# Two more weight pairs in the front stage, joint block scores, and one sample step per unit in an encoder step

## The chip, the cores and the metric

The kernel runs on one core of a Trainium2 chip. The metric is the device time of one execution in microseconds; lower is better. All arithmetic is fp32; products that need accuracy are made of fp32r halves (a high part and a low part of each operand, three matmuls for a product).

## The reference

One step of a one-layer streaming encoder on 1024 prompt positions and 8 samples of 16 positions (T = 1152 rows, D_MODEL = 1024). Cut to what this change touches:

```python
h = rmsnorm(x, g_pre_mix)
qa, ka, va, qb, kb, vb, ga, gb = project(h, w_in)   # h @ w_in: 34 column tiles of 128
# prompt: per chunk of 64 positions, band attention with bias (and sink in branch A)
oa = prompt_band(qa, ka, va, 128, bias_a, sink)     # window 128, 8 heads, 2 kv heads
ob = prompt_band(qb, kb, vb, 512, bias_b, None)     # 8 chunks back, 8 heads
# samples: 16 new positions on a cache of 128
oa_s = sample_band(qa_s, ka_s, va_s, cache_a, bias, sink)
ob_s = sample_band(qb_s, kb_s, vb_s, cache_b, bias, None)
merged = sigmoid(ga) * (oa @ w_oa) + sigmoid(gb) * (ob @ w_ob)
```

After it come the output projection, a gated MLP with a width-3 convolution, and norms. Those stages are not touched.

## The kernel before, in words

**Front stage.** The rows of x are normalised and transposed into xk, and h @ w_in is begun. Two column tiles of w_in form a pair (list `pairs`, L196): one pair is a 2x2 block product (two tiles, two halves of the contraction, two halves of the rows) that `head`/`Away`/`head_back` and `tail` (L440 to L477) compute with seven half-size products instead of eight. A product is two row chunks of 288 columns, four contraction steps and three matmuls, 24 matmuls, so a pair is 7 x 24 = 168 matmuls of 288 columns. There are ten pairs. The first seven (`NA`) have their first two products made early (class `Away`, L222). For each operand `split_left` (L171) runs one copy on ScalarE and one subtraction on VectorE; results go to `in_dr` in HBM by `store`.

**Attention stage** (L489 to L870). The 14 column tiles that no pair holds are computed here as dense work: `dense_pieces` (L525) cuts a tile into three pieces of 384 columns, a piece into four quanta of six matmuls (24 per piece, 72 per tile). Between them stand the eight units, one pair of heads each: units 0 to 3 are branch A (two key blocks of 128 per query block), units 4 to 7 branch B (up to five). A unit has six steps: four prompt steps ("p") of two query blocks, and after the second of them two sample steps ("s"), one for each half of the samples.

A step runs in a pipeline with the one before it. Its scores (`scores` L636, `sample_scores` L723) go out first; VectorE adds the bias and takes the minimum (L666), ScalarE takes the exponent (L671), VectorE normalises (L682, L686). Meanwhile TensorE makes the transposes of the step before (L703, into two PSUM tiles `pt`, each copied out by ScalarE L707 or VectorE L705), then its products with V (`values` L712). `spread` (L812) puts the quanta of dense work between these parts, by `share` (L831) and by `pieces_per_unit` (L823): 4 pieces in units 0 to 3, then 6, 6, 6, 5. The parts of a prompt step are: first score block, two transposes, two transposes, rest of the scores and the normalising, transposes, rest, and the late transposes of samples:

```python
items = [step(sc), step(tr, 2), step(tr, 2), rest(sc), step(tr, 2), rest(tr), lates]
upto = quanta * share[i] // share[-1]
spread(items, dense, upto - done)
```

`scores` yields after each of its two query blocks (L675), so that transposes and dense work stand between the two. `fetch(u + 1)` (L602) loads the rows of the next unit at step i == 3 (L836); its splits (L557 to L561) run on ScalarE and VectorE. All loads and stores are issued from one queue (SP). A scheduler at compile time follows the order of the program and lets an engine take a later instruction where it believes that an earlier one is not ready; on the chip each engine then runs its list in order. The score tiles in PSUM are two (`pss`), of two banks each.

A sample step loads half a K cache and half a V cache (L737 to L740, one buffer each), makes 16 score matmuls (16 records), softmax on 128 x 144, two transposes (L769, L770), ten value records (L778, L781), a copy, and one step later a late transpose and a store (L785).

## Time and profile before

| | |
|---|---|
| three runs | 1658.04, 1662.12, 1663.2 us, median 1662.12 |
| the profiled execution | 1666.81 us |
| its span, first to last instruction | 1665.0 us |
| mean granted TensorE clock | 0.991 |
| TensorE matmul, weight load | 97%, 89% of the span |
| VectorE, ScalarE, GpSimd | 65%, 44%, 13% |
| DMA | 206.47 MB, mean 124 GB/s |

The profile is of one execution. Matmul records overlap, and their ends are modelled, so a time is best read from one start to the next. The attention stage begins at 256 us of the span and ends at about 616 us.

### The profile page before, as it was taken

To read this page: it belongs to the slowest core of one execution; us is meant where nothing else is said; L and a number is where in the kernel's file an instruction comes from. 1 tells how busy PE (TensorE), PEld (TensorE's weight loads), DVE (VectorE), ACT (ScalarE), POOL (GpSimd) and SP (SyncE) were. 2 spreads that over 40 slices of the span, in tenths; PEclk is the share of its full clock that TensorE was granted. 3 is DMA by queue.
4 is the path that set the end of the run, shared out by engine and by line. 5 is a ranking of instruction groups with operands and counts; after the bars stand their busy time and mean duration, and the time that the engine had idled before them with its cause. 6 is when DMAs were issued, how large, how long until landed. Compare 5 with 4: busy or idle time off the path is not lost. (4 is left out here: it accounts for less than half of the span.)

```text
span 1665.0 us, 27771 instructions
## 1 busy us (share of the span) xinstructions
PE 1609.2 (97%) x10839; PEld 1480.8 (89%) x10839; DVE 1086.8 (65%) x2009; ACT 726.6 (44%) x1417; POOL 223.8 (13%) x297
## 2 busy tenths in 40 slices
PE   6999999999999999999999999999999998999997
PEld 6999998788888889978898999999999997888886
DVE  6965546665665546454397766766666675965986
ACT  7511235565454445332373344444444444534342
POOL 1000011111111103411002211111111110000003
PEclk9999999999999999999999999999999999999999
DMA  7743326445333236442254311221221129053023
GB/s 256 246 167 143 113 83 208 141 142 163 121 116 119 72 126 229 135 161 94 76 188 128 118 64 70 80 80 71 75 80 67 68 68 339 2 194 128 1 94 134
DMA packets 95364, 206.47 MB, mean 124 GB/s; under 512 B 21704, under 2 KB 46072, under 8 KB 95232
## 3 DMA queue, kind: packets, MB, share of 16 engines
q1 hardware_dynamic: 95232, 204.69, 36.2%
q8 instruction: 85, 1.39, 0.3%
q14 instruction: 47, 0.39, 0.1%
HBM read 148.13 MB, written 61.24 MB: 126 GB/s over the span
## 5 line engine op out<-in xcount | busy, mean ns | idle before, releaser
L143 PE MATMUL x<-xot,s 128*128 128x288 f32 x1152 | 157.7, 295 | 0.9 <-DVE w L1144 0.9
L143 PEld LDWEIGHTS x<-xot,s 128*128 128x128 f32 x1152 | 154.9, 188 | 1.1 <-ACT a L1007 1.1
L1354 PE MATMUL x<-wbp,zap 128*128 128x512 f32 x576 | 135.3, 389 | 0.0
L1354 PEld LDWEIGHTS x<-wbp,zap 128*128 128x128 f32 x576 | 108.1, 188 | 22.4
L1007 ACT ACTIVATE s<-uw 128x512 fp32r<-128x512 f32 x96 | 60.1, 626 | 96.1 <-issue 41.7
L1354 PE MATMUL p<-wbp,zap 128*128 128x512 f32 x432 | 102.0, 393 | 0.0
L1354 PEld LDWEIGHTS p<-wbp,zap 128*128 128x128 f32 x432 | 82.2, 190 | 17.2
L1008 DVE TENSOR_TENSOR s<-uw,s 128x512 fp32r<-128x512 f32 x96 | 68.9, 718 | 32.3 <-ACT s L1007 32.3
L1185 DVE SCALAR_TENSOR_TENSOR wk<-w,cw,wk 128x128 f32<-128x128 f32 (+2 forms) x144 | 83.0, 613 | 9.9 <-ACT wk L1183 9.1
L671 ACT ACTIVATE p<-p,m 128x256 f32<-128x256 f32 (+4 forms) x128 | 74.9, 588 | 33.0 <-DVE m L666 33.0
L143 PE MATMUL x<-xob,s 128*128 128x288 f32 x576 | 82.6, 299 | 6.3 <-DVE wk L1144 6.3
L143 PEld LDWEIGHTS x<-xob,s 128*128 128x128 f32 x576 | 79.6, 191 | 6.9 <-ACT s L1007 2.6
L1008 DVE TENSOR_TENSOR a<-uw,a 128x512 fp32r<-128x512 f32 x62 | 42.8, 691 | 63.6 <-ACT a L1007 62.4
L143 PE MATMUL z<-xot,s 128*128 128x288 f32 x576 | 80.7, 295 | 0.0
L143 PE MATMUL z<-xot,a 128*128 128x288 f32 x576 | 80.7, 295 | 0.0
L143 PEld LDWEIGHTS z<-xot,s 128*128 128x128 f32 x576 | 78.1, 188 | 0.0
L143 PEld LDWEIGHTS z<-xot,a 128*128 128x128 f32 x576 | 78.1, 188 | 0.0
L143 PE MATMUL ix<-t,s_i 128*128 128x288 f32 x480 | 65.6, 295 | 0.3 <-DVE iu L188 0.3
L143 PEld LDWEIGHTS ix<-t,s_i 128*128 128x128 f32 x480 | 64.3, 188 | 0.5 <-issue 0.5
L143 PE MATMUL x<-xob,a 128*128 128x288 f32 x456 | 63.9, 295 | 0.0
L143 PE MATMUL y<-xob,a 128*128 128x288 f32 x456 | 63.9, 295 | 0.0
L143 PEld LDWEIGHTS x<-xob,a 128*128 128x128 f32 x456 | 61.8, 188 | 0.0
(657 smaller groups left out, 3890.9 us busy)
## 6 DMA issues: line engine op xcount, KB each, us to landing
uw<-in_w_upg SPq DMA_DIRECT2D x53, 512.0 KB, 4.5
iw<-in_w_in SPq DMA_DIRECT2D x27, 512.0 KB, 4.6
gg<-in_dr SPq DMA_DIRECT2D x16, 576.0 KB, 3.9
in_dr<-gt SPq DMA_DIRECT2D x42, 192.0 KB, 1.9
z_dr<-wk SPq DMA_DIRECT2D x24, 256.0 KB, 2.1
z_dr<-wk SPq DMA_DIRECT2D x24, 224.0 KB, 1.9
xt<-in_x SPq DMA_DIRECT2D x9, 512.0 KB, 9.9
oT<-o_dr SPq DMA_DIRECT2D x8, 576.0 KB, 7.1
```

What stands on the lines that cost most here:

```text
L143: nc.tensor.matmul(ps, w[:, i, k], right(j, c, k), start=first and n == 0, stop=last and n == len(todo) - 1, skip_group_check=True)
L671: nc.scalar.activation(p[h][:, 0:n], p[h][:, 0:n], AF.Exp, bias=least[h], scale=-1.0, accum_out=st.d[:, h, i:i + 1])
L1007: nc.scalar.activation(sp[:, 0], src, AF.Copy)
L1008: nc.vector.tensor_tensor(sp[:, 1], src, fr(sp[:, 0]), op=ALU.subtract)
L1185: nc.vector.scalar_tensor_tensor(out, src(t), cw[:, f, t:t + 1], out, op0=ALU.mult, op1=ALU.add)
L1354: nc.tensor.matmul(ps, z[:, i, k, c], w[:, j, k], start=first and n == 0, stop=last and n == 2, skip_group_check=True)
```

## The change

Tiles 6, 7 and 11, 15 leave the dense list and become two more pairs of the front stage (fifth and sixth of twelve). `dense_tiles` keeps ten tiles, 30 pieces, of which the units get 3, 3, 3, 3, 4, 4, 4, 3 and the end of the stage three, as before. `scores` no longer yields between the two query blocks, except after the first one where the keys take two chunks (third and fourth prompt steps of units 4 to 7). The two sample steps of a unit become one step, with the same matmuls, softmax operations for each half, and buffers that hold both halves: four cache tiles from three buffers, one PSUM tile for the transposes and one for the values, one copy of each. `fetch(u + 1)` stands at i == 2, ahead of the sample step. The output tile `oo` of the prompt steps has one buffer instead of two.

```diff
-        pairs = [(4, 5), (0, 1), (2, 3), (10, 14)] + [(18 + n, 26 + n) for n in range(6)]
+        pairs = [(4, 5), (0, 1), (2, 3), (10, 14), (6, 7), (11, 15)] + [(18 + n, 26 + n) for n in range(6)]
...
                 st.k0.append(k0)
-                yield
+                if i == 0 and nch > 1:
+                    yield
+            yield
...
-            o = pp.tile([P, 256], F32, name=f"oo{st.name}", tag="oo")
+            o = pp.tile([P, 256], F32, name=f"oo{st.name}", tag="oo", bufs=1)
...
-        def sample_scores(st, u, half):
+        def sample_scores(st, u):
...
-            kt = sm.tile([P, 4, P], F32, name=f"kc{st.name}", tag="kc", bufs=1)
-            nc.sync.dma_start(kt[:], kc[ci, half])
-            st.v = sm.tile([P, 4, P], F32, name=f"vc{st.name}", tag="vc", bufs=1)
-            nc.sync.dma_start(st.v[:], vc[ci, half])
+            kt, st.v = [[sm.tile([P, 4, P], F32, name=f"{n}{st.name}_{half}", tag="cache", bufs=3) for half in range(2)]
+                        for n in ("kc", "vc")]
+            for src, tiles in ((kc, kt), (vc, st.v)):
+                for half in range(2):
+                    nc.sync.dma_start(tiles[half][:], src[ci, half])
...
+            for half in range(2):
+                for i in range(4):
+                    b = half * 4 + i
...
+                    nc.tensor.matmul(ps[r, half, 0:P], q, kt[half][:, i], start=True, stop=True)
+                    nc.tensor.matmul(ps[r, half, P:144], q, k.kn[:, b * SS:(b + 1) * SS], start=True, stop=True)
...
+            pt = pst.tile([P, 2, 2, P], F32, name=f"t{st.name}", tag="pt")
+            for half in range(2):
+                nc.tensor.transpose(pt[:, half, 0], st.p[:, half, 0:P], ident[:])
+                nc.tensor.transpose(pt[:, half, 1], pms[half][:], ident[:])
...
-        dense_tiles = [6, 11, 15, 7, 12, 16, 8, 13, 17, 9, 24, 32, 25, 33]
+        dense_tiles = [12, 16, 8, 13, 17, 9, 24, 32, 25, 33]
...
-        pieces_per_unit = [4, 4, 4, 4, 6, 6, 6, 5]
+        pieces_per_unit = [3, 3, 3, 3, 4, 4, 4, 3]
...
-            order = [("p", 0), ("p", 1), ("s", 0), ("s", 1), ("p", 2), ("p", 3)]
-            share = [3, 5, 7, 9, 13, 17] if u < 4 else [3, 6, 8, 10, 14, 18]
+            order = [("p", 0), ("p", 1), ("s", None), ("p", 2), ("p", 3)]
+            share = [3, 5, 8, 12, 16] if u < 4 else [3, 6, 9, 13, 17]
...
-                if i == 3 and u < 7:
+                if i == 2 and u < 7:
                     fetch(u + 1)
```

## Rows read from the trace of the kernel before

**Rows 1.** The page's first part: busy us, share of the span, instructions.

```profile
PE 1609.2 (97%) x10839; PEld 1480.8 (89%) x10839; DVE 1086.8 (65%) x2009; ACT 726.6 (44%) x1417; POOL 223.8 (13%) x297
```

**Rows 2.** Windows, attention stage: length; busy PE, PEld, DVE, ACT, POOL; clock, DMA, GB/s.

```profile
256.00:616.00 360.00, 353.51 (x2821) 296.66 (x2820) 220.78 (x781) 181.06 (x510) 42.39 (x54) 1.00 0.40 126
```

**Rows 3.** Timeline, TensorE, end of the front stage: start, duration, instruction, count.

```profile
249.67 3.35 PE L143 MATMUL ix<-xk,s_i 128*128 128x288 f32 x24
252.86 3.35 PE L143 MATMUL iz<-t,a_i 128*128 128x288 f32 x24
256.05 0.34 PE L117 MATMUL d<-xk,w6s 128*128 128x384 f32 x1
...
257.78 0.34 PE L118 MATMUL d<-xk,w6s 128*128 128x384 f32 x1
```

**Rows 4.** Windows, single units (1, 2 and 7), columns as in rows 2.

```profile
290.80:327.90 37.10, 34.78 (x280) 28.66 (x278) 22.45 (x90) 19.97 (x66) 5.03 (x12) 0.95 0.45 134
327.90:360.60 32.70, 32.70 (x280) 27.59 (x278) 21.75 (x88) 19.52 (x65) 4.04 (x6) 1.00 0.44 141
...
552.40:598.80 46.40, 46.38 (x384) 38.76 (x382) 29.29 (x102) 22.34 (x56) 2.39 (x1) 1.00 0.18 58
```

**Rows 5.** Timeline, TensorE, pieces of steps in units 1, 2 and 4.

```profile
313.74 0.39 PE L663 MATMUL s<-kah,q1h 64*128 64x256 f32 x2
...
314.29 0.33 PE L769 MATMUL ts<-ident,ps 128*128 128x128 f32 x1
...
329.72 0.45 PE L117 MATMUL d<-xk,w15s 128*128 128x384 f32 x1
...
342.97 0.45 PE L745 MATMUL sss<-kcs,qbd 128*32 128x128 f32 x8
...
343.40 0.33 PE L769 MATMUL ts<-ident,ps 128*128 128x128 f32 x1
...
343.59 0.42 PE L117 MATMUL d<-xk,w7s 128*128 128x384 f32 x1
...
345.76 0.38 PE L778 MATMUL os<-vtna,pcs 128*128 128x128 f32 x2
346.07 0.42 PE L781 MATMUL os<-vcs,pcs 128*32 128x128 f32 x8
346.43 0.38 PE L663 MATMUL s<-kah,q2h 64*128 64x256 f32 x2
...
358.34 0.42 PE L117 MATMUL d<-xk,w7s 128*128 128x384 f32 x1
...
425.91 0.42 PE L663 MATMUL s<-k4h,q4h 64*128 64x320 f32 x2
...
426.98 0.45 PE L117 MATMUL d<-xk,w8s 128*128 128x384 f32 x1
```

**Rows 6.** Timeline, second prompt step of unit 2: scores, minimum, exponent, sink, normalising.

```profile
333.25 0.39 PE L663 MATMUL s<-kah,q2h 64*128 64x256 f32 x2
...
333.91 0.48 DVE L666 CUSTOM_DVE_ANT_0 p<-s,bt,sinkb 128x256 f32<-128x256 f32 x1
...
335.04 0.50 ACT L671 ACTIVATE p<-p,m 128x256 f32<-128x256 f32 x1
...
337.01 0.47 ACT L680 ACTIVATE se<-m,sinkp 128x2 f32<-128x2 f32 x2
...
337.93 1.14 DVE L686 TENSOR_SCALAR p<-p,dn 128x256 f32<-128x256 f32 x4
```

**Rows 7.** Timeline, two waits of TensorE and the load behind the first.

```profile
288.53 0.32 SPq L549 DMA_DIRECT2D k4raw<-in_dr  x1
...
294.13 0.63 ACT L557 ACTIVATE k4h<-k4raw 128x512 fp32r<-128x512 f32 x1 [3.74 <-DMA k4raw<-in_dr]
...
296.06 0.58 PE L703 MATMUL pt<-ident,p 128*128 128x128 f32 x2 [2.32 <-ACT pk L707]
...
448.22 0.66 PE L703 MATMUL pt<-ident,p 128*128 128x128 f32 x4 [2.47 <-DVE oo L720]
```

**Rows 8.** DMA issues of the attention stage: stores of `oo`, KB each, us to landing.

```profile
o_dr<-oo SPq DMA_DIRECT2D x32, 128.0 KB, 2.9
```

## Prediction

> **What bounds the kernel now.** I read the page's busy shares first: TensorE is busy for 97% of the span, VectorE for 65%, ScalarE for 44% [rows 1]. Then the windows by stage: in the 360 us of the attention stage TensorE is busy for 353.51 us, its weight loads for only 296.66, VectorE for 220.78, ScalarE for 181.06 [rows 2]. So the stage is TensorE's, but the records overlap, and "busy" hides what passes between two kinds of matmuls. The timeline shows it: dense matmuls follow each other every (257.78 - 256.05) / 10 = 0.173 us [rows 3], so twelve should take 2.08 us, but a visit of twelve lasts from 343.59 to 345.76, 2.17 us [rows 5]. Six score matmuls (three pairs of 256 columns, 0.12 us each by the pitch inside the group) take 313.74 to 314.29, 0.55 us [rows 5]: about 0.2 us of it is the change of operand shape. Every visit to another kind of work costs TensorE 0.1 to 0.2 us in which it counts as busy.

> [...]

> **The change part by part**, against the profiled execution (1665.0 us of span, 1666.8 in all, 4.7 us above the median of the runs).

> *Two more pairs.* Dense, two pairs are four tiles of 72 matmuls: 288 x 0.173 = 49.8 us. In the front stage they are 2 x 168 matmuls; a product of 24 lasts 252.86 - 249.67 = 3.19 us, so 2 x 7 x 3.19 = 44.7 us [rows 3]. Net **-5.1 us**. Their splits on ScalarE and VectorE, loads and stores lie beside the products as those of the ten pairs do; rows 3 show products back to back to the last. Were this cover gone, it would show there as pitch.

> *Joint scores.* Two groups of 0.55 us become one. The nearest joint group is that of two chunks of 320 columns, 425.91 to 426.98, 1.07 us [rows 5]; with 2 x 64 columns less per matmul pair I estimate 0.9 us for 256. That saves 0.2 us a step (bounds: nothing, and 0.3 if the second group cost only its pitch). Units 0 to 3 have four such steps, 0.8 us each unit, units 4 to 7 two, 0.4 us.

> *One sample step.* Scores: 0.43 us a half [rows 5], of which the pitch inside is some 0.1 to 0.2; joint about 0.6, saving 0.25. Values: 0.67 us a half (345.76 to 346.43 [rows 5]); joint about 0.9, saving 0.4. Transposes cost the same. **0.65 us** a unit (bounds 0.3 and 0.8). Softmax operations are as many; ScalarE copies, the reciprocal and the sink terms are halved, a fraction of a us off the path.

> *Fewer visits of dense work.* Unit 2 has 14 visits (the first at 329.72, the last at 358.34 [rows 5]). The program's order alone gives 10 (one in each of the first four steps, three in each of the last two); the compiler's reordering added four. After, with five steps, no break between the score blocks and 12 quanta instead of 16, the program's order gives 6; I take 8, and in units 4 to 7 five fewer by the same count. At 0.1 us: 0.6 and 0.5 us a unit.

> Sum of the merging: 4 x (0.8 + 0.65 + 0.6) + 4 x (0.4 + 0.65 + 0.5) = **-14.4 us**. Gross with the pairs: -19.5.

> *What it costs.* The dense work is also the cover of the softmax chain. In unit 2 the chain from the first score to the last normalising is 333.25 to 337.93 + 1.14 = 339.07, 5.8 us; ScalarE's four exponents (0.5 us apart) and the sink terms set its end more than the second block's scores do [rows 6], so joint scores shorten it little. The unit takes 32.7 us over six steps [rows 4], 5.4 each. After: 32.7 - 4 x 6 x 0.173 (one piece) - 2.05 = 26.5 us over five, 5.3 each. The second prompt step is left with one quantum and about 4 us of TensorE work; the transposes that need its result come after the sample scores, some 0.9 us too early. The compiler can pull quanta of the sample step forward (the four added visits above are of that kind), at 0.1 to 0.2 us for each extra visit. The four minima of a step now stand together on VectorE, 0.4 us apart, and a copy of transposes queued behind them on VectorE makes the third `pt` tile wait. I take **1 us a unit, +7** in all (one unit ends the stage); bounds 0 and 2.5. VectorE rises from 21.75 of 32.7 us [rows 4] to about 21.5 of 27.5, 78%; it does not become the bound, and unit 7, with 20 quanta instead of 24, ran its 46.4 us with TensorE busy for 46.38 [rows 4].

> *One buffer of `oo`.* The copy must now wait for the store before it, issued at once and landed 2.9 us later [rows 8]; steps are 4 us apart at least. Nothing, up to 0.5 us a unit when the store lands late; it is inside the 7. Behind the waiting copy on VectorE stand the minima of the next step, so the same bound holds for TensorE.

> *The fetch and the sample loads.* The fetch moves ahead of the eight bias and four cache loads of the sample step; in time it stays the sample step plus two prompt steps before its unit. No loads are added, and cache loads have three buffers for four tiles, so only the second V half waits for a score group, a step before it is read. What matters is a load that lands later than the compiler thought: the keys for unit 4, issued at 288.53, held ScalarE until 294.13, and TensorE, waiting for ScalarE's copy of `pt`, stood 2.32 us [rows 7]. [...] One such event costs 4.4 us; a second one, of 2.47 us, is at 448.22. They can vanish or grow in number: +-5 us, taken as 0.

> Total: -19.5 + 7 = -12.5. From the profiled 1666.8 this gives 1654; from the median 1662.1 it gives **1649.5 us**.

> **The rivals.**
> *A, nothing new waits.* The gross gain stays, and one or both late loads go: -19.5 to -25, 1637 to 1643. For it: a list scheduler with 12 free quanta a unit has enough to fill 1 us. Against: every step has less of it.
> *B, only the arithmetic counts.* If TensorE at 97% is full, no visit costs anything and only the pairs pay: -5.1, 1657. [...]
> *C, the chain takes over (slower).* The front stage grows by 44.7 us for certain; the attention stage must give that up, and gross it gives 49.8 + 14.4 = 64.2. The place is the transposes of each prompt step, waiting for the normalising 5.8 us after its scores and for the two `pt` tiles. From 19.5 us of waits on, 0.5 us in each of the 40 steps, the change loses; with 0.7 us in each (28 us) it is +8.5, **1671 us**. For it: the two longest waits of the stage are of this kind [rows 7]. Against: they had a late load behind them, and VectorE and ScalarE have idle time in every unit.
> [...] No row here shows scores waiting for a tile.
> *D, the pairs don't pay.* Seven products at the front cost what eight dense ones did, by loads or splits that fall behind, and the merging is lost in extra visits: 0, 1662. Against: the even 3.19 us [rows 3].

> **How the numbers follow.** Forecast 0.50 (1643 to 1656, from waits of 0.2 to 1.7 us a unit), A 0.17, B 0.12, C 0.13, D 0.08. Runs of this kernel differ by 0.3%, 5 us, and less can't be told from no change. Forecast and A are faster; B lies on that line and is halved; C is slower, D the same: faster 0.73, same 0.14, slower 0.13. The range, 1637 to 1662, takes in the forecast, A, B and half of D, and leaves out C.

> **What the profile would show.** Right: dense work starts at about 301 us and the stage ends near 604, 303 us long; twelve score matmuls in about 0.9 us and 32 sample score records in about 0.6; eight dense visits in unit 2 for 14; VectorE's share of the stage above 70%; waits of TensorE in it below 15 us. Wrong: long waits at the transposes behind L686, L707 or L705, or behind `oo`; a granted clock below 0.98 in the stage; products of the front further apart than 3.19 us.

## The result, and the profile after

The changed kernel takes **1643.74 us** (four runs, 1642.28 to 1648.29) beside 1662.11 for the kernel before on the same chip: ratio 0.9897, 95% interval 0.988 to 0.9915, 18 us less. The forecast was 1649.5: faster, as said, but by half as much again. In the experiments a gain in us beside a ratio is that ratio's share of the 1662 us before, which can differ by up to 2 us from the difference of two medians. The profiled execution took 1648.29 us with a span of 1646.5, 18.5 us under that of the kernel before. Both profiled executions lie 4.6 to 4.7 us above the median of their runs, so the two traces can be set against each other as they stand.

The first part of the page after, and the row of a DMA queue, q8, that becomes important later (packets, MB, share):

```profile
PE 1591.7 (97%) x10887; PEld 1471.5 (89%) x10887; DVE 1096.0 (67%) x2015; ACT 726.1 (44%) x1411; POOL 215.9 (13%) x293
...
q8 instruction: 85, 1.39, 0.3%
```

TensorE has 48 matmuls more than in [rows 1], which is 2 x 168 - 288. The windows of the attention stage and of the up-projection stage, columns as in rows 2:

```profile
300.00:603.73 303.73, 292.61 (x2535) 244.26 (x2533) 210.88 (x754) 167.62 (x478) 34.09 (x51) 1.00 0.43 138
...
819.07:1372.10 553.03, 540.23 (x4044) 538.64 (x4042) 392.61 (x619) 257.96 (x483) 103.26 (x145) 1.00 0.29 96
```

The same windows of the kernel before:

```profile
256.05:619.23 363.18, 354.07 (x2824) 296.89 (x2822) 221.85 (x782) 183.60 (x514) 42.39 (x54) 1.00 0.40 128
...
832.96:1391.10 558.14, 543.07 (x4043) 541.66 (x4041) 392.78 (x618) 257.47 (x483) 102.77 (x145) 0.99 0.28 95
```

So the front stage gives 300.0 - 256.0 = +44.0 us, the attention stage 303.7 - 363.2 = -59.5, and everything behind it -3.0, of which the up-projection stage, which the change does not touch, has -5.1. How far such differences hold is seen in the traces of the experiments below. The attention stage repeats within 0.8 us where the code is the same (363.2, 363.7 and 363.5 us before; 303.7, 303.8 and 304.0 after). The front stage, where its start is not delayed, varies more: 252.4 to 256.1 us in six traces with ten pairs, 297.4 to 300.0 in five with twelve, 44.5 apart in the mean.

The end of the front stage (timeline, TensorE), which answers to [rows 3]:

```profile
293.66 3.35 PE L143 MATMUL ix<-xk,s_i 128*128 128x288 f32 x24
296.84 3.35 PE L143 MATMUL iz<-t,a_i 128*128 128x288 f32 x24
300.03 0.34 PE L117 MATMUL d<-xk,w12s 128*128 128x384 f32 x1
```

The products still follow each other every 3.18 to 3.19 us. Pieces of steps in unit 1, which answer to [rows 5]:

```profile
336.23 0.39 PE L663 MATMUL s<-kah,q1h 64*128 64x256 f32 x2
...
337.14 0.87 PE L705 MATMUL pt<-ident,p 128*128 128x128 f32 x6
...
338.99 0.45 PE L749 MATMUL sss<-kcs,qbd 128*32 128x128 f32 x8
...
339.71 0.45 PE L117 MATMUL d<-xk,w16s 128*128 128x384 f32 x1
...
350.94 0.60 PE L786 MATMUL os<-vtna,pcs 128*128 128x128 f32 x4
...
352.04 0.39 PE L663 MATMUL s<-kah,q1h 64*128 64x256 f32 x2
```

Twelve score matmuls take 337.14 - 336.23 = 0.91 us, where two groups of 0.55 stood; the 32 records of the sample scores 0.72, where two halves of 0.43 stood; the values 1.10, where two of 0.67 stood.

The waits of TensorE in the attention stage after (us in total, times, longest):

```profile
PE pt L705 <- ACT pk L709: 2.7, 6, 0.7
PE o L720 <- ACT pk L709: 2.7, 4, 1.4
PE pt L705 <- DVE pk L707: 2.4, 1, 2.4
PE ts L777 <- DVE pm L768: 0.5, 1, 0.5
```

They sum to 8.3 us against 6.4 before. No row is behind `oo`, and none has scores waiting for a tile. The most regular of them is the third `pt` tile, here in unit 1:

```profile
331.86 0.40 ACT L671 ACTIVATE p<-p,m 128x128 f32<-128x128 f32 x1 [1.01 <-DVE m L666]
...
332.64 0.58 ACT L709 ACTIVATE pk<-pt 128x512 f32<-128x512 f32 x1
...
333.27 0.44 PE L705 MATMUL pt<-ident,p 128*128 128x128 f32 x2 [0.67 <-ACT pk L709]
```

ScalarE waits for the first minima, takes two exponents, and only then copies the `pt` tile that TensorE needs emptied. This is the place of rival C, at 0.67 us and not in every step. The longest wait, 2.42 us, has another origin:

```profile
417.05 3.49 DVE L561 SCALAR_TENSOR_TENSOR q5l<-q5raw,q5h 128x512 fp32r<-128x512 f32 x2
417.30 2.69 POOL L104 TENSOR_TENSOR w9s<-w9r,w9s 128x1024 fp32r<-128x1024 f32 x1 [1.33 <-issue]
...
422.04 0.44 PE L705 MATMUL pt<-ident,p 128*128 128x128 f32 x2 [2.42 <-DVE pk L707]
```

Two query splits, elsewhere 0.69 us each, take 3.49 us while GpSimd subtracts a weight tile, and the minima and the `pk` copy stand behind them on VectorE. Taken singly, the first lasted its usual 0.68 us; the second, begun at 417.65, lasted 2.89 us and ended 0.55 us after the subtraction, as if it had stood still until GpSimd was done.

Single units after (units 1 and 2), columns as in rows 4:

```profile
330.32:358.35 28.03, 27.24 (x254) 22.93 (x253) 21.22 (x86) 18.86 (x63) 4.90 (x12) 1.00 0.56 168
358.35:386.47 28.12, 27.11 (x254) 23.13 (x252) 20.14 (x85) 17.52 (x61) 4.38 (x7) 1.00 0.51 158
```

Unit 2 came to 28.12 us, not 27.5; unit 1 fell from 37.10 [rows 4] to 28.03, at a granted clock of 1.00 instead of 0.95.

### The profile page after: what moved, and what is told of

It reads as the page before. It is cut to its first block, busy times and chain, and to the rows that moved or that the text cites. A ratio compares the mean times of both kernels' runs of the same rounds, so it can differ in the third digit from the quotient of the medians.

```text
span 1646.5 us, 27860 instructions
## 1 busy us (share of the span) xinstructions
PE 1591.7 (97%) x10887; PEld 1471.5 (89%) x10887; DVE 1096.0 (67%) x2015; ACT 726.1 (44%) x1411; POOL 215.9 (13%) x293
## 5 line engine op out<-in xcount | busy, mean ns | idle before, releaser
L143 PE MATMUL ix<-t,s_i 128*128 128x288 f32 x576 | 78.6, 295 | 0.3 <-DVE iu L188 0.3
L143 PEld LDWEIGHTS ix<-t,s_i 128*128 128x128 f32 x576 | 77.2, 188 | 0.5 <-issue 0.5
L173 ACT ACTIVATE s_i<-iw 128x512 fp32r<-128x512 f32 x48 | 30.3, 630 | 88.4 <-PE ix L143 49.0
## 6 DMA issues: line engine op xcount, KB each, us to landing
z_dr<-wk SPq DMA_DIRECT2D x24, 256.0 KB, 2.1
xt<-in_x SPq DMA_DIRECT2D x9, 512.0 KB, 10.1
```

Source lines behind the costliest of these rows:

```text
L143: nc.tensor.matmul(ps, w[:, i, k], right(j, c, k), start=first and n == 0, stop=last and n == len(todo) - 1, skip_group_check=True)
L173: nc.scalar.activation(sp[:, 0], src, AF.Copy)
```

## The experiments

Each is compared with the kernel before on the same chip. First the parts of the change one by one.

**The pairs alone**, on the old units:

```diff
-        pairs = [(4, 5), (0, 1), (2, 3), (10, 14)] + ...
+        pairs = [(4, 5), (0, 1), (2, 3), (10, 14), (6, 7), (11, 15)] + ...
-        dense_tiles = [6, 11, 15, 7, 12, 16, ...]
-        pieces_per_unit = [4, 4, 4, 4, 6, 6, 6, 5]
+        dense_tiles = [12, 16, ...]
+        pieces_per_unit = [3, 3, 3, 3, 4, 4, 4, 3]
```

> The twelve pairs, ten dense tiles and 27 + 3 dense pieces alone, on the old six-step units (two sample steps, a yield after each score block). Theory 'the parts add up': the pairs give 5.1 us on TensorE (front +44, dense work -50) and the shorter cover costs 0 to 5 us of new waits at the transposes, so 1657 to 1662, ratio 0.997 to 1.000. Rival 'the pairs bring the gain': most of the 18 us comes with the pairs, ratio below 0.993 (under 1651). Rival 'the old steps need the cover': ratio above 1.002.

1653.34 us, ratio 0.9944 (0.9929 to 0.9959), -9.3 us: more than the theory and less than its rival had said. But the trace gives the pairs only a part of that: the front stage ends at 298.2 and the attention stage lasts 315.4 us, so both together are 613.6 against 619.2 before. The rest lies behind them: the up-projection stage lasts 550.3 us instead of 558.1, with the same instructions. That asked for the last six experiments.

**The joint scores alone**: only the `yield` of `scores` is moved.

```diff
                 st.k0.append(k0)
-                yield
+                if i == 0 and nch > 1:
+                    yield
+            yield
```

> Only the yield between the two score blocks is gone; ten pairs, six steps, old buffers. Theory 'the parts add up': 24 joint groups save 0.19 us each (4.6 us) and about 24 dense visits of 0.1 us go, less some new waits for the pt tiles: -4 to -7 us, 1655 to 1658, ratio 0.996 to 0.9975; joint groups of 256 columns last 0.91 us. Rival 'the copies behind the four minima eat it': waits of TensorE at the pt tiles grow by 4 us or more, ratio 0.999 to 1.002.

1655.74 us, 0.996 (0.9946 to 0.9974), -6.6 us. The attention stage lasts 355.3 us, 7.9 less. Unit 1 alone fell from 37.1 to 32.1, so the late load of [rows 7] no longer stops TensorE: ScalarE comes to the split of those keys 4.7 us after their load was issued, and does not wait. The rest of the stage gave 2.8 us, less than the 4.8 of the arithmetic, though its visits of dense work fell from 137 to 127.

**The one sample step alone**: the new `sample_scores` and its followers, `fetch` at i == 2, one buffer of `oo` and the five-step `share` lists; pairs, dense tiles, pieces and yields as before.

```diff
-            order = [("p", 0), ("p", 1), ("s", 0), ("s", 1), ("p", 2), ("p", 3)]
+            order = [("p", 0), ("p", 1), ("s", None), ("p", 2), ("p", 3)]
...
```

> Only the sample step made one (with its buffers, one oo buffer, five steps, the fetch at the third step, the share lists of after with the old 4 and 6 pieces); ten pairs, a yield after each score block. Theory 'the parts add up': 32 score records in 0.72 us instead of 2 x 0.42, 20 value records in 1.11 instead of 2 x 0.67, eight steps fewer with one or two dense visits each: -3 to -6 us, 1656 to 1659, ratio 0.9965 to 0.998. Rival 'the larger lump blocks': single oo buffer and one long softmax make TensorE wait, ratio at or above 1.000.

1661.91 us, 1.0003 (0.9989 to 1.0016): nothing, as the rival had said, but hardly for its reason: the two long waits of TensorE, 2.9 and 2.2 us, stand where the kernel before had 2.3 and 2.5. Units 2 and 3 last 32.7 and 34.5 us, as before; unit 0 gains 2.1 and unit 1 loses 1.1 again to the late load, which is still there (timeline of this kernel, then its window with the granted clock):

```profile
288.92 0.63 ACT L557 ACTIVATE k4h<-k4raw 128x512 fp32r<-128x512 f32 x1 [4.28 <-DMA k4raw<-in_dr]
...
290.67 0.69 PE L703 MATMUL pt<-ident,p 128*128 128x128 f32 x2 [2.92 <-DVE pk L705]
```

```profile
280.00:300.00 20.00, 17.08 (x110) 13.97 (x111) 11.23 (x41) 8.92 (x30) 1.26 (x6) 0.83 0.47 150
```

TensorE stood for 2.92 us, and the granted clock of those 20 us is 0.83.

In the kernel after the same load holds ScalarE for 0.44 us only:

```profile
335.29 1.15 ACT L557 ACTIVATE k4h<-k4raw 128x512 fp32r<-128x512 f32 x2 [0.44 <-DMA k4raw<-in_dr]
```

**Joint scores and one sample step, without the new pairs** (the two edits above together):

> Joint scores and one sample step together, without the two new pairs (ten pairs, 14 dense tiles, 4 and 6 pieces). Theory 'the parts add up': the sum of the two single edits, -8 to -13 us, 1649 to 1654, ratio 0.992 to 0.995; the attention stage is shorter by that and the front stage unchanged. Rival 'pairs and merging need each other': less than half of the 18 us (ratio above 0.9945) here and in the pairs alone. Rival 'merging is all of it': ratio 0.990 or below, with the full cover of dense work still there.

1651.69 us, 0.9939 (0.992 to 0.9959), -10.1 us. The window of its attention stage:

```profile
253.20:604.10 350.90, 341.71 (x2823) 294.78 (x2821) 216.77 (x754) 176.14 (x494) 42.05 (x54) 1.00 0.41 132
```

12.3 us less than before. Unit 2 lasts 31.5 us, 1.2 less; unit 1 5.6 less. The sample step, worth nothing alone, gives 355.3 - 350.9 = 4.4 us of this stage on top of the joint scores. ScalarE does not wait for the keys of unit 4 here either. From here to the kernel after, the stage gets 47.2 us shorter, 2.6 short of the 49.8 that the dense work takes.

**Two further pairs**, fourteen in all, on the kernel after: tiles 12, 16 and 13, 17 become pairs, and six dense tiles are left.

```diff
+        pairs = [..., (6, 7), (11, 15), (12, 16), (13, 17)] + ...
...
-        pieces_per_unit = [3, 3, 3, 3, 4, 4, 4, 3]
+        pieces_per_unit = [2, 2, 2, 2, 2, 2, 2, 1]
```

> After with two pairs more, (12, 16) and (13, 17): 14 pairs, six dense tiles, two pieces a unit (one in the last), three at the end. Theory 'the parts add up, cover still there': front +44.7, dense work -50, new waits 1 to 4 us, so front and attention stage together shrink by 1 to 4 us against after (603.7 us to the end of the attention stage). Rival 'the chain takes over' (C of the prediction): with 8 quanta a unit the transposes wait for the normalising and for the pt tiles in most steps, waits of TensorE in the attention stage above 20 us, and the two stages together grow by more than 5 us. The late stages may move by some 7 us either way by the fetch phase, so the stages are compared, not the totals alone.

1660.99 us, 0.9996 (0.9985 to 1.0008). The front stage grows by 42.7 us, as before, but the attention stage gives up only 27.2 of 49.8. Its window, and two of its waits:

```profile
342.70:619.20 276.50, 261.44 (x2248) 200.24 (x2246) 209.85 (x754) 159.82 (x462) 24.16 (x46) 0.99 0.43 137
```

```profile
PE ts L777 <- DVE pm L768: 2.6, 1, 2.6
...
PE s L663 <- DVE m L666: 1.7, 6, 0.5
```

Here the chain has taken over: VectorE is busy for 76% of the stage, and there are waits at every link of it, among them six where scores wait for the minima that free their tile, of which the kernel after had none. Named waits sum to only 12 us, not above 20 as the rival had said. The trace also has its work in smaller pieces: the score matmuls stand in 86 groups instead of 45, and a visit of dense work has 5.2 matmuls in the mean instead of 6.8. That the rest of the 22.6 us lost lies there is likely, but was not measured by itself.

**The low halves of the dense weights on VectorE instead of GpSimd**, on the kernel after:

```diff
-        box["w"] = weight_tile(w_in[col], f"w{col}")
+        box["w"] = weight_tile(w_in[col], f"w{col}", "scalar", "vector")
```

> After with the low halves of the dense weights made on VectorE instead of GpSimd (ten subtractions of 1.2 us more on VectorE, none of 2.4 to 2.7 us on GpSimd in the attention stage). Theory 'the two engines slow each other': the query split of 3.49 us beside GpSimd's subtraction at 417 us returns to 1.4, the wait of 2.42 us at the transposes after it goes, the attention stage is 0 to 4 us shorter, ratio to before 0.987 to 0.990. Rival 'VectorE is short of time': 12 us more on it bring waits at the transposes, the stage is 2 to 6 us longer, ratio 0.991 to 0.994.

1644.24 us, 0.9898 (0.9879 to 0.9917): as the kernel after. The wait of 2.4 us behind the query splits is gone (the longest of `pt` is 1.2), but VectorE has 216.4 us of work in place of 210.9, and the stage lasts 305.1 us against 303.7, where 0 to 4 us less were expected. The two query splits now take 1.28 us together instead of 3.49, so it was the subtraction on GpSimd that had held them up; by what means, no trace shows. The wait was worth removing, the work was not worth moving.

**The late stage.** This is the up-projection stage; its instructions are the same in every kernel here. SP's queue at some of its first loads (start, us, count), before and after:

```profile
911.64 2.37 SPq L1192 DMA_DIRECT2D w<-c_dr  x3
...
931.56 2.61 SPq L1192 DMA_DIRECT2D w<-c_dr  x3
```

```profile
879.19 1.35 SPq L1204 DMA_DIRECT2D w<-c_dr  x3
...
886.60 2.16 SPq L1140 DMA_DIRECT2D a<-a_dr  x2
894.09 0.32 SPq L1222 DMA_DIRECT2D z_dr<-wk  x1
...
896.64 1.36 SPq L1204 DMA_DIRECT2D w<-c_dr  x3
```

Three issues take 1.35 us after, but 2.37 and 2.61 before; one of the three is over a microsecond longer. What differs is when a packet of the queue q8 runs. In a window at the long issue before, and in one after (packets, MB, share):

```profile
q8 instruction: 1, 0.02, 8.4%
```

```profile
q8 instruction: 1, 0.02, 4.2%
```

The first is 911.6 to 912.6, on the issue; the second 889 to 891, where SP has nothing to issue. The page has 85 such packets for 2 x 10887 matmuls and weight loads, 256 for each, and in the up-projection stage 256 of TensorE's instructions start from one packet to the next in the median, before as after: so q8 brings TensorE's instruction list (kernels with 2 x 10967 have 86 packets). The pairs lengthen that list by 96 matmuls and weight loads ahead of the late stages, and so move every later fetch. The long issue reaches TensorE by a chain of waits (kernel before): ScalarE waits for the rows that it loads, VectorE for ScalarE, and TensorE for a sum that stands behind that on VectorE.

```profile
915.42 1.15 ACT L1183 ACTIVATE wk<-w,cb,cw 128x448 f32<-128x448 f32 x2 [2.85 <-DMA w<-c_dr]
916.21 0.69 DVE L1185 SCALAR_TENSOR_TENSOR wk<-w,cw,wk 128x448 f32<-128x448 f32 x1 [2.92 <-ACT wk L1183]
917.41 2.96 PE L143 MATMUL x<-xob,s 128*128 128x288 f32 x11 [2.37 <-DVE wk L1144]
```

The first 127 us of the stage, before and after:

```profile
832.96:960.00 127.04, 117.89 (x856) 116.72 (x855) 103.95 (x162) 60.40 (x100) 22.07 (x31) 0.97 0.45 142
```

```profile
819.07:946.11 127.04, 120.06 (x894) 118.71 (x893) 108.30 (x167) 63.03 (x104) 25.88 (x35) 1.00 0.47 146
```

After, TensorE is 38 matmuls further in the same time, at a granted clock of 1.00 instead of 0.97. Its waits there sum to 9.1 us before and 6.9 after; those that differ, before and then after:

```profile
PE x L143 <- DVE wk L1144: 6.3, 3, 2.4
```

```profile
PE x L143 <- DVE w L1156: 1.5, 1, 1.5
PE x L143 <- ACT wk L1195: 1.4, 1, 1.4
PE x L143 <- ACT s L1019: 1.2, 1, 1.2
```

To test this, idle matmuls were put at the very start, to shift the list and nothing else. First form: 24 (96 instructions) in the kernel before, 40 (160) in the kernel after.

```diff
+            warm = psz.tile([P, 512], F32, name="warm", tag="ps")
+            for _ in range(24):
+                nc.tensor.matmul(warm[:, 0:8], ident[:], ident[:, 0:8], start=True, stop=True)
             b = []
```

> The kernel before with 24 tiny extra matmuls (identity by eight of its columns, into a PSUM tile that nothing reads) at the very start, where TensorE waits for the first rows: 96 more instructions on TensorE, no other work. Theory 'fetch phase': the late stages run faster with the two pairs because TensorE's instruction list is longer by about 96 and its fetches no longer fall on the loads w<-c_dr of the up-projection stage; so this kernel gains what the pairs alone gained beyond 3 us: the stretch from that stage's first matmul to the down-projection falls from 556-558 to 550-553 us, in all -4 to -8 us, ratio 0.995 to 0.9975. Rival 'it is something the pairs do' (rows in memory, DMA traffic): the stretch stays at 556-558 us, ratio 0.9985 to 1.0015.

> The kernel after with 40 of the same tiny matmuls (160 instructions on TensorE), which brings its instruction list at the up-projection stage to the place, modulo 256, that the joint merging without pairs had. Theory 'fetch phase': the waits of 2 to 3 us at 65, 85 and 106 us into that stage come back, the stretch to the down-projection grows from 550-553 to 556-558 us, and the time rises by 4 to 8 us over after: ratio to before 0.992 to 0.995. Rival 'it is something the pairs do': ratio 0.9885 to 0.991, as after.

The kernel before with 96: 1662.71 us, 1.0005 (0.9993 to 1.0016); its up-projection stage fell to 551.0 us. The kernel after with 160: 1660.19, 0.9994 (0.9981 to 1.0006), its stage rose to 556.9. The stage did what was expected both times. Both totals missed what was expected, and say little, because the idle matmuls were slow (timeline of the first):

```profile
1.34 10.41 PE L312 MATMUL warm<-ident 128*128 128x8 f32 x48 [1.34 <-POOL ident masks.py:199]
11.60 3.52 PE L286 MATMUL tp<-ident,xn 128*128 128x128 f32 x16
```

The first transposes start at 11.6 us instead of 7.8, in the second kernel at 18.4. The second form loads only 8 columns and splits the idle matmuls over two places where TensorE waits for VectorE anyway:

```diff
+            for _ in range(16):
+                nc.tensor.matmul(warm[0:8, 0:8], ident[:, 0:8], ident[:, 0:8], start=True, stop=True)
             b = []
...
                 b[1].transposed()
+                for _ in range(8):
+                    nc.tensor.matmul(warm[0:8, 0:8], ident[:, 0:8], ident[:, 0:8], start=True, stop=True)
```

These are the 24 of a shift by 96; a shift by 160 has 24 and 16. The start of the first:

```profile
1.34 0.95 PE L312 MATMUL warm<-ident 128*8 128x8 f32 x32 [1.34 <-POOL ident masks.py:199]
7.86 1.97 PE L286 MATMUL tp<-ident,xn 128*128 128x128 f32 x8 [5.56 <-DVE xn L278]
```

With these the start is not delayed. Four kernels were shifted: before, merged without pairs, after, and pairs alone (96, 96, 160 and 160 instructions).

> The kernel before with 24 extra fp32 matmuls of 8 x 8 on TensorE (96 instructions), 16 ahead of the first transposes and 8 after the second block's, where TensorE waits for VectorE anyway; their results are not used. Theory of the fetch (TensorE's instruction list is fetched in blocks of 256 instructions, and where a fetch falls on a DMA issue of SP, that issue takes 1.0 to 1.7 us instead of 0.43, and the load comes late): 131 + 96 = 227 into a block when the up-projection stage starts, close to the kernel after (212), so the stage lasts 551 to 553 us instead of 558, the first loads of that stage are issued in under 0.6 us each, and the whole is 5 to 7 us faster, ratio 0.9955 to 0.997. Rival (the late stage gains only from what the pairs changed ahead of it): stage of 556 to 558, ratio 0.999 to 1.001. In the earlier form with 128 x 8 matmuls the start was 3.8 us late; here the first transposes should start by 8.5 us.

> The joint scores and the one sample step without the two new pairs, with the same 24 extra matmuls of 8 x 8 (results not used): 116 + 96 = 212 into a block, as in the kernel after. Theory of the fetch: up-projection stage of 550 to 553 us instead of 557.8, and the whole 5 to 7 us under the 1651.7 of the same kernel without them: 1645 to 1647, ratio to the kernel before 0.9895 to 0.991. Then the pairs themselves are worth 1 to 4 us, and about half of what they gave alone (9.3 us) was where the fetches fell. Rival (the pairs are worth 9 us by themselves): stage of 556 to 558, ratio 0.993 to 0.995.

> The kernel after with 40 extra fp32 matmuls of 8 x 8 (160 instructions, results not used), 24 ahead of the first transposes and 16 after the second block's: 212 + 160 = 372, 116 into a block, as in the merging without pairs. Theory of the fetch: the up-projection stage lasts 555 to 558 us instead of 550 to 553, with long issues (over 1 us) of its first loads and waits of 1.5 to 2.9 us on TensorE, and the whole loses 5 to 7 us: 1648 to 1652, ratio to the kernel before 0.9925 to 0.995, if the start is not delayed. Rival: the extra matmuls cost only their own time, 1 to 3 us where they outlast VectorE's wait: stage of 550 to 553, ratio 0.989 to 0.991.

> The two new pairs alone, on the old units of six steps, with 40 extra matmuls of 8 x 8 (160 instructions, results not used): 222 + 160 = 382, 126 into a block, where the kernel before stands (131). Theory of the fetch: up-projection stage of 555 to 559 us instead of 550.3, with issues over 1 us at the loads of a, z_dr and w; the three shifts so far moved the time by 1.8, 3.8 and 6 us, so the ratio goes from 0.9944 to between 0.9955 and 0.998 (1653 to 1658 beside 1661). Rival (the gain of the pairs alone does not hang on the fetches): stage of 550 to 553, ratio 0.9935 to 0.9955.

They took 1661.30, 1648.20, 1651.11 and 1659.02 us. Ratios to the kernel before (interval in brackets), by where the up-projection stage starts in a block of 256 instructions, and that stage's length in the profile. The place is the number of TensorE's matmuls, weight loads and semaphore instructions in the trace ahead of the stage, less whole blocks; in the four shifted kernels it came out one less than expected:

| | at 115 to 131 | at 211 to 226 |
|---|---|---|
| before | 1; 558.1 us | 0.9989 (0.9977 to 1.0002); 551.8 |
| pairs alone | 0.9988 (0.9977 to 0.9999); 555.5 | 0.9944 (0.9929 to 0.9959); 550.3 |
| merging alone | 0.9939 (0.992 to 0.9959); 557.8 | 0.9916 (0.9899 to 0.9934); 551.7 |
| both | 0.9933 (0.9916 to 0.9951); 559.4 | 0.9897 (0.988 to 0.9915); 553.0 |

In every row the right column is the faster one, by 1.8, 7.3, 3.8 and 6.0 us, 4.7 in the mean (in the first row within the interval of nothing, in the third the two intervals overlap a little), whether the idle matmuls were added on the left or on the right. Three stage lengths came as the theory of the fetch had said, and the fourth, 559.4 us for the kernel after, lies beyond the 555 to 558 expected. Of the totals only that of the kernel after came as expected: the kernel before and the merged one moved less, the pairs alone more. SP's rows go with it: the merged kernel shifted to 211, then the kernel after shifted to 115:

```profile
877.92 1.37 SPq L1209 DMA_DIRECT2D w<-c_dr  x3
```

```profile
896.75 2.69 SPq L1209 DMA_DIRECT2D w<-c_dr  x3
```

The other traces say the same. Seven of the fourteen kernels here start the stage at 115 to 131: they have three to five issues of SP over 0.9 us in its first 127 us, each on a packet of q8, and the stage lasts 555.5 to 559.4 us. The other seven have one or none, and it lasts 549.0 to 553.0 us.

The rival, that the late stage gains from what else the pairs change, has fallen: the merged kernel has no new pairs, and 24 idle matmuls give it the short stage; the kernel after has them, and 40 idle matmuls take it away. Why a fetch for TensorE holds up an issue of SP was not tried and stays open; when it does is told in the last section. Nor is it known why the kernel before gains only 1.8 us in its runs where its profiled stage is 6.3 us shorter. A part is the spread of executions: its profiled execution lies 4.7 us above the median of its runs, that of its shifted form 2.2 below.

## Why the prediction was right, and where it was not

**Right in sign and in place.** Dense work was to start at 301 us and starts at 300.03. The stage was to end near 604; that was reckoned from an end at 616 us, where the last dense matmul stands before (its record ends at 616.6), and by the same mark it ends at 601.1. The 603.73 used above is the first matmul of the next stage, at 619.23 before, so its nearness to 604 is chance. Front and attention together are -15.5 us in the trace, where -12.5 was forecast, and the rest, -3.0, was in no step. From like to like in the table, the change is worth 0.9933 on the left (-11 us) and 0.9897 / 0.9989 = 0.9908 on the right (-15 us): the forecast of -12.5 lies between them. What it missed is the fetch, because each stage not touched was taken as unchanged. That the change lands in the faster column is luck: nothing in it aims at that.

**The pairs (-5.1).** The rows of the table without them against those with them differ by 2.0, 7.5, 1.0 and 3.2 us, 3.4 in the mean. The front term was right (+44.0 in the two traces, +44.5 over all, for 44.7). The dense term was 49.8 in arithmetic, 47.2 on the merged units and 47.8 on the old ones. Rival D, that the pairs do not pay, was close on the left of the table; rival B had the sizes the wrong way round, since the merging is worth 0.0059 in the mean, 9.8 us. Rival A, nothing new waits, has its edge at 1643 us, nearer to the result than the forecast's 1649.5; but only half of it came true: the late loads went, and new waits came.

**Joint scores (-0.2 each).** Two groups of 0.55 us became 0.91: 0.19 saved. The 1.07 of the two chunks of 320 was the right neighbour [rows 5]. That the joint scores would also free unit 1 of its late load was in the text as +-5, taken as 0. The 4.4 us that one late load was put at are units 1 and 2 of [rows 4], 37.10 - 32.70; with the joint scores alone, where that load holds nothing, unit 1 lasts 32.1.

**One sample step (-0.65 a unit).** Mis-sized: scores 0.86 to 0.72 us, values 1.34 to 1.10, 0.38 in all, just above the lower bound. I estimated 0.6 and 0.9 without a row of that shape. By itself the step gave nothing.

**Fewer visits (14 to 8 in unit 2).** Counted in the timeline it is 11; the compiler cuts the dense work more often than I took. In the whole stage visits fell from 137 to 106, 31 where 44 had been taken.

**New waits (+7, 1 us a unit, bounds 0 and 2.5).** The sum came out near because two errors met. Against the gross gain of each unit (6.2 us in units 0 to 3, 9.85 in the others), units 0, 2, 3, 4 and 7 fell short by 1.8, 1.6, 1.1, 3.5 and 1.7 us, 9.6 in all or 1.9 a unit, twice what I took. Units 1, 5 and 6, where before had late loads, gained 2.9, 1.8 and 0.2 more than that gross gain. Together +4.7 for +7. So the middle of the range for waits was too low, and the late loads, taken as nothing, went.

**One buffer of `oo`** cost nothing: no wait in the stage is on its store, which lands after 2.8 us, as in [rows 8].

**VectorE** has 210.88 / 303.73 = 69% of the stage; I had said above 70.

**Rival C** is real, one step further on. With fourteen pairs the front stage took 42.7 us more and the attention stage gave up only 27.2, so 22.6 of the 49.8 were lost, and the time went back to that of the kernel before, though the up-projection stage is a short one there (551.9 us). That joint scores take both score tiles at once costs nothing in the kernel after, where no scores wait for a tile; with fourteen pairs six waits for one sum to 1.7 us.

## What to carry to other kernels

Work that fills the waits of a chain can be moved away only until the chain shows: here moving the first four tiles lost 2.6 us of 49.8, the next four 22.6. When a stage that the change does not touch gets faster, compare its lines with the same stage in another variant before crediting the change: a shift of the instruction list by a few idle matmuls tells the two apart in one run. And measure each part alone and together, since the sample step gave 0 alone and 4.4 us of its stage with the joint scores.

## What was not expected of the hardware

In the up-projection stage three to five issues are held, or one or none, since a fetch comes every 256 instructions (in its first 127 us every 16.9 to 18.6 us after, 16.7 to 21.7 before) and the loads of w recur about as often (every 15.4 to 17.5 us after, 14.8 to 20.0 before). With issues held, the kernel before has waits of TensorE of up to 2.4 us and a granted clock of 0.97 over those 127 us; where the stage starts in the block is worth 4.7 us of 1650 in the mean of the table.
